# Two banks of one double PSUM tile are read once both are written, and the gate rows and residual pieces are loaded earlier, in the feed-forward block of a two-layer diffusion trunk

## The chip, the cores and the metric

The kernel runs on one core of a Trainium2 chip. The metric is the device time of one execution in microseconds (us). The engines are TensorE (PE), VectorE (DVE), ScalarE (ACT) and GpSimd (POOL); SyncE (SP) issues most of the DMA loads, and ACT's queue issues some.

## The reference

A trunk of two layers works on 512 latent rows and 256 context rows of width 1024. Each layer has mixers, an output projection and a layer norm, and then the block that this change is about:

```python
f = channel_mlp(modulate(x, m[3], m[4]), w_ff1[l], w_ff2[l])     # square(relu(h @ w1)) @ w2, 1024 -> 4096 -> 1024
x = layer_norm_affine(DN_ALPHA * x + m[5] * f, ln2_g[l], ln2_b[l])
```

Here `m[5]` is a gate vector, one value for each of the 1024 columns. Layer 0 does the same for the context rows with a gate of their own; in layer 1 the context rows need no feed-forward block. All of it is float32.

## The kernel before, in words

A float32 matmul is done as three matmuls of rounded halves (`mm3`, line 133: hi·hi, lo·hi, hi·lo), so every operand is split in two: ACT copies the high half, DVE subtracts to get the low half. The names are `hiw`/`low` for weights, `fop` for the halves of an operand of the second matmul, `hh`/`hl` for the normalised input.

**The chunks.** The 4096 hidden columns go in eight chunks of 512. In layer 0 the rows are 768 (latent and context), in layer 1 they are 512. In chunks 0 to 6 the product with `w_ff2` is done by a scheme with seven half-sized products in place of eight: `operands` makes the seven left sides (POOL sums, then `fop` halves by ACT line 1269 and DVE line 1270), `weights` the seven right sides (POOL differences line 1295, halves by ACT line 1290 and DVE line 1291), and `product(i, ...)` multiplies. A product fills HT banks of PSUM, 128x512 each (HT is 3 in layer 0, 2 in layer 1), with six matmuls a bank. Each bank is then added into one or more quadrants of the result, `acc` or `base`, by DVE (line 1340); the first time a quadrant is touched, ACT copies it (line 1343).

**The banks.** Products 0, 2, 4 and 6 use single-bank tiles (`PA`, three buffers). Products 1, 3 and 5 use a double tile `P2` of two banks (two buffers, shared with the `ff1` tiles), and in layer 0 one bank `PF` besides. The framework tracks who reads and writes a tile as a whole: in a double tile, the first matmul into the second bank stands behind the reads of the first.

**The order of the work.** TensorE's order is written by hand. Each letter f is one `ff1` tile of the next chunk (24 matmuls of 512 columns, in layer 0 another 24 of 256 columns), each digit one product:

```python
order = "f01f23f45f6" if c < NCH - 2 else "01f23f456ff"
```

The other engines and the DMA queues run in the order that the framework's scheduler gave them. Each works strictly through its own list: what stands behind a waiting instruction waits too.

**The end of a layer's block (the tail).** After chunk 6 the gate rows are loaded (`rows2(0)`, on ACT's DMA queue, one row spread over 128 partitions) into pool G (four buffers). Then, for each of the six (four) 128x1024 tiles of `acc`: POOL multiplies by the gate (line 1422), DVE adds the residual rows `rawx` (line 1423), loaded from the DRAM copy `xr` into the raw pool (four buffers of 512 KB, which the weights use too). Then chunk 7 is done the plain way: `square` makes `fh`, `fl` from the hidden rows, `ff2_w` loads and splits the last weights of `w_ff2` (lines 163, 166), `ff2_tile` multiplies, DVE takes the bank times the gate (`fft`, line 1366), POOL adds it to `acc` (line 1367), and `done` does the layer norm (lines 181, 343, 345) and, in layer 0, makes the input halves `hh`, `hl` of the next layer, whose first products are `wb`.

Of the kernel before, what the change touches and what calls it, by code (L numbers as in the profile page):

```python
# [9 lines left out]
F32 = mybir.dt.float32  # L10
F32R = mybir.dt.float32r
AF = mybir.ActivationFunctionType
ALU = mybir.AluOpType
# [7 lines left out]
LT = NL // 128  # L21
# [26 lines left out]
class Trunk:  # L48
# [1133 lines left out]
    def ffn(self, l, hL, hC, x, xc, rows2, mod2, done):  # L1182
        nc, A = self.nc, self.A
        w1 = A["w_ff1"][l].rearrange("(k p) n -> p k n", p=128)
        w2 = A["w_ff2"][l].rearrange("(f p) n -> p f n", p=128)
        NCH = DFF // 512
# [7 lines left out]
        def ff1_mm(o, h, t0, W):  # L1194
            t1 = t0 + o.shape[-1]
            for k in range(KT):
                self.mm3(o, W[k], [t[:, t0:t1] for t in h[k]], k == 0, k == KT - 1)
# [4 lines left out]
        def square(r, n):  # L1202
            hi, lo = self.Z("fh"), self.Z("fl")
            nc.scalar.activation(out=hi[:, :n], in_=r[:, :n], func=AF.Square)
            nc.vector.tensor_tensor(out=r[:, :n], in0=r[:, :n], in1=r[:, :n], op=ALU.mult)
            nc.vector.tensor_tensor(out=lo[:, :n], in0=r[:, :n], in1=hi[:, :n].bitcast(F32), op=ALU.subtract)
            return hi, lo

        N = NL + NC if full else NL
        half = N // 2  # L1210
        HT = half // 128

        def ff1_tile(f, spare):

            W = ff1_w(f, spare)
            ps = self.P2("ff1")
            ff1_mm(ps[:, :NL], hL, 0, W)
            if full:
                ff1_mm(ps[:, NL:NL + NC], hC, 0, W)
            r = self.T("relu", 768)  # L1220
            relu(r, 0, ps[:, :N])
            return r
# [57 lines left out]
        def weights(c):  # L1280
# [28 lines left out]
        TO = (("11", "B"), ("12",), ("11",), ("12", "22"), ("B",), ("21", "22"), ("21",)) if full else (  # L1309
            ("11",), ("12",), ("2",), ("22",), ("6",), ("7",), ("21",))  # L1310

        def place(acc, base, q, t):
            if len(q) == 1:
                return base[q][t]
            n = int(q[1]) - 1
            return acc[HT * (int(q[0]) - 1) + t][:, 512 * n:512 * n + 512]

        def product(i, B, left, acc, base, seen):

            if i in (0, 2, 4, 6):
                banks = [self.PA("ff2") for _ in range(HT)]
            else:
                big = self.P2("ff2")
                banks = [big[:, 0:512], big[:, 512:1024]]
                if HT > 2:
                    banks.append(self.PF("ff2"))
            W = next(B)
            for t in range(HT):  # L1330
                ps = banks[t]
                for p in range(2):
                    self.mm3(
                        ps, [h[:, 128 * t:128 * t + 128] for h in left[p][i]],
                        [h[:, p, :] for h in W], p == 0, p == 1,
                    )
                for q in TO[i]:
                    sl = place(acc, base, q, t)
                    if (q, t) in seen:
                        nc.vector.tensor_tensor(out=sl, in0=ps, in1=sl, op=ALU.add)  # L1340
                    else:
                        seen.add((q, t))
                        nc.scalar.activation(out=sl, in_=ps, func=AF.Copy)

        def ff2_w(c, n):
            return [
# [22 lines left out]
        rs = ff1_first()  # L1369

        xr = self.pd.tile([N, D], F32, name=self.nm("xr"), tag=self.nm("xr"))
        for j, t in enumerate(x + (xc or [])):
            nc.sync.dma_start(out=xr[128 * j:128 * j + 128, :], in_=t)
        acc = [self.X([128, 1024], "acc") for _ in range(N // 128)]
        base = {}
# [8 lines left out]
        seen = set()  # L1384
        self.pin = True
        for c in range(NCH - 1):
            B = weights(c)
            rs, nxt = [], []
            order = "f01f23f45f6" if c < NCH - 2 else "01f23f456ff"
            for o in order:  # L1390
                if o != "f":
                    product(int(o), B, left, acc, base, seen)
                    continue
                rs.append(ff1_tile(4 * c + 4 + len(rs), True))
                if c < NCH - 2 and len(rs) % 2 == 0:
                    nxt.append(operands(*rs[-2:]))
            left = nxt
        self.pin = None

        gl, gc = rows2(0)  # L1400

        def plus(o, a):
            nc.vector.tensor_tensor(out=o, in0=o, in1=a, op=ALU.add)
# [9 lines left out]
            plus(c21, p7)  # L1413
            plus(c22, p7)
        for j, t in enumerate(acc):
            raw = self.pr.tile([128, 1024], F32, name=self.nm("rawx"), tag="raw")
            self.load(out=raw, in_=xr[128 * j:128 * j + 128, :])
            for n in range(2):
                if full and (j >= HT or n):
                    sl = t[:, 512 * n:512 * n + 512]  # L1420
                    nc.vector.tensor_tensor(out=sl, in0=sl, in1=base["B"][j % HT], op=ALU.add)
            nc.gpsimd.tensor_tensor(out=t, in0=t, in1=gl if j < LT else gc, op=ALU.mult)
            nc.vector.tensor_tensor(out=t, in0=t, in1=raw, op=ALU.add)
        rows2(1)
        fs = [square(r, N) for r in rs]
        tiles = [(128 * j, t, gl if j < LT else gc) for j, t in enumerate(acc)]
        Ws = [ff2_w(NCH - 1, n) for n in range(2)]
        self.ends = []
# [239 lines left out]
```

## Time and profile before

| what | value |
|---|---|
| median of the 2 runs shown | 1746.6 us (1743.52 to 1749.68) |
| the profiled execution | 1759.88 us, span 1758.0 us |
| busy over the span | PE 86%, DVE 60%, ACT 40%, POOL 29% |
| mean granted TensorE clock | 0.936 of full speed |
| chunks 0 to 6, layer 0 | 450 to 966.6 us |
| tail, layer 0 | 966.6 to 1034.5 us |
| chunks 0 to 6, layer 1 | 1350 to 1699.5 us |
| tail, layer 1 | 1699.5 to 1758 us |

The profiled execution is 13.3 us longer than the median of the runs. TensorE is the busiest engine, so the time goes where its idle time is, and where its clock is below full speed (the two levels are 2.4 and 1.2 GHz; a value between 0.5 and 1 is a mix over the stretch).

### The profile page before, as it was taken

The numbers are of one execution on the slowest core, as the hardware profiler recorded it, in microseconds if no ns is written. First come the engines' busy times: TensorE is split into PE (matmuls) and PEld (weight loads), VectorE is DVE, ScalarE is ACT, GpSimd is POOL, SyncE is SP. The second block draws the span as 40 slices with busy tenths as digits, with TensorE's granted clock in tenths as the row PEclk, the third lists the DMA queues.
The fourth block names the chain that finished last, engine by engine and source line by source line (L and its number), as shares of the span: only waits on it lengthen the run. The fifth ranks groups of instructions, "written<-read, shape, count | busy, mean of one in ns | idle before, by whom it ended". The sixth has DMA issues, their size and how long they took to land.

```text
span 1758.0 us, 23844 instructions
## 1 busy us (share of the span) xinstructions
PE 1511.0 (86%) x9228; PEld 1245.6 (71%) x9228; DVE 1046.3 (60%) x1773; ACT 697.8 (40%) x1267; POOL 507.9 (29%) x422
## 2 busy tenths in 40 slices
PE   5899898999888988988889499988989898888865
PEld 4788777878777777877767377877767676666644
DVE  3394556475545455465554788576565556666567
ACT  4444455335532233233221165355445543343312
POOL 1011442232231213213220631153233432334323
PEclk9999999999998999999989699999989999999987
DMA  8432564542112121121110523245460332322122
GB/s 294 127 111 76 164 199 150 200 155 72 62 46 84 37 60 61 48 60 48 61 60 12 191 97 85 85 157 168 156 210 13 108 95 84 96 74 83 60 72 83
DMA packets 150952, 180.42 MB, mean 103 GB/s; under 512 B 9096, under 2 KB 96568, under 8 KB 150840
## 3 DMA queue, kind: packets, MB, share of 16 engines
q1 hardware_dynamic: 140792, 160.42, 29.0%
q10 hardware_dynamic: 10048, 18.49, 3.1%
q8 instruction: 72, 1.18, 0.3%
q14 instruction: 40, 0.33, 0.1%
HBM read 169.43 MB, written 9.46 MB: 102 GB/s over the span
## 4 chain that ended last, share of the span: by engine, by line
PE 57%; DVE 18%; issue 8%; POOL 7%; ACT 5%; DMA 4%; SPq 0%; POOLq 0%; DVEq 0%; ACTq 0%
PE ff L133 29%; PE wo L133 6%; PE wb L133 3%; DVE acc L1340 3%; POOL raww L1295 3%; DVE fop L1270 2%; DVE low L1291 2%; PE o L133 2%; PE ada L133 2%; PE wa L133 2%; PE pT L189 2%; PE wp L133 2%; DMA wada<-in_w_ada 2%; PE wu L133 2%; ACT hiw L1290 2%
## 5 line engine op out<-in xcount | busy, mean ns | idle before, releaser
L133 PE MATMUL ff<-hiw,fop 128*128 128x512 f32 x980 | 356.4, 430 | 109.5 <-DVE acc L1340 84.0
L133 PEld LDWEIGHTS ff<-hiw,fop 128*128 128x128 f32 x980 | 203.4, 208 | 177.1 <-DVE acc L1340 99.3
L1291 DVE TENSOR_TENSOR low<-raww,hiw 128x1024 fp32r<-128x1024 f32 x98 | 137.4, 1404 | 217.6 <-ACT hiw L1290 217.6
L1295 POOL TENSOR_TENSOR raww<-raww,raww 128x1024 f32<-128x1024 f32 x56 | 142.3, 2542 | 349.9 <-DMA raww<-in_w_ff 117.8
L133 PE MATMUL ff<-hh,hiw 128*128 128x512 f32 (+1 forms) x672 | 239.2, 356 | 0.0
L133 PE MATMUL ff<-hl,hiw 128*128 128x512 f32 (+1 forms) x672 | 238.1, 354 | 0.0
L133 PE MATMUL ff<-hh,low 128*128 128x512 f32 (+1 forms) x672 | 238.0, 354 | 0.0
L1290 ACT ACTIVATE hiw<-raww 128x1024 fp32r<-128x1024 f32 x98 | 103.6, 1059 | 306.5 <-PE ff L133 306.4
L133 PE MATMUL ff<-low,fop 128*128 128x512 f32 x490 | 207.7, 424 | 0.0
L1340 DVE TENSOR_TENSOR acc<-ff,acc 128x512 f32<-128x512 f32 x228 | 152.3, 685 | 67.8 <-PE ff L133 65.0
L133 PEld LDWEIGHTS ff<-hh,hiw 128*128 128x128 f32 x672 | 128.3, 191 | 19.4
L133 PEld LDWEIGHTS ff<-hl,hiw 128*128 128x128 f32 x672 | 128.0, 190 | 19.2
L133 PEld LDWEIGHTS ff<-hh,low 128*128 128x128 f32 x672 | 127.2, 189 | 18.1
L163 ACT ACTIVATE hiw<-raww 128x1024 fp32r<-128x1024 f32 x64 | 67.9, 1061 | 163.7 <-PE ff L133 122.1
L1270 DVE TENSOR_TENSOR fop<-relu,fop 128x384 fp32r<-128x384 f32 (+1 forms) x140 | 80.9, 605 | 65.3 <-ACT fop L1269 65.3
L133 PEld LDWEIGHTS ff<-low,fop 128*128 128x128 f32 x490 | 102.1, 208 | 19.5
L166 DVE TENSOR_TENSOR low<-raww,hiw 128x1024 fp32r<-128x1024 f32 x64 | 87.6, 1369 | 35.1 <-ACT hiw L163 35.1
L548 POOL TENSOR_SCALAR p<-p,rec 128x768 f32<-128x768 f32 (+3 forms) x80 | 63.4, 796 | 140.6 <-DVE rec L547 131.3
L1269 ACT ACTIVATE fop<-relu 128x384 fp32r<-128x384 f32 (+1 forms) x140 | 58.3, 460 | 82.5 <-POOL relu L1277 82.1
L1274 POOL TENSOR_TENSOR fsum<-relu,relu 128x384 f32<-128x384 f32 (+1 forms) x28 | 25.4, 907 | 208.6 <-ACT relu L1261 208.6
L133 PE MATMUL ada<-wada,sc 128*32 128x128 f32 x1536 | 62.8, 302 | 21.0 <-DMA wada<-in_w_ada 21.0
L1200 ACT ACTIVATE relu<-ff 128x768 f32<-128x768 f32 (+2 forms) x76 | 45.4, 606 | 73.9 <-PE ff L133 73.8
(365 smaller groups left out, 3219.9 us busy)
## 6 DMA issues: line engine op xcount, KB each, us to landing
raww<-in_w_ff SPq DMA_DIRECT2D x120, 512.0 KB, 4.1
wada<-in_w_ada SPq DMA_DIRECT2D x96, 512.0 KB, 4.4
rawwo<-in_w_out SPq DMA_DIRECT2D x16, 512.0 KB, 6.4
rawx<-xr SPq DMA_DIRECT2D x10, 512.0 KB, 3.3
rawz<-in_w_ff SPq DMA_DIRECT2D x8, 512.0 KB, 4.8
xr<-x SPq DMA_DIRECT2D x8, 512.0 KB, 7.2
rawwb<-in_w_in SPq DMA_DIRECT2D x12, 256.0 KB, 3.8
gate<-grow ACTq DMA_DIRECT2D x6, 512.0 KB, 7.6
```

Of the source, the lines that this page charges most:

```text
L133: return self.pinned(self.nc.tensor.matmul(out, lhsT, rhs, start=start, stop=stop))
L163: i = nc.scalar.activation(out=hi, in_=raw, func=AF.Copy)
L166: nc.vector.tensor_tensor(out=lo, in0=raw, in1=hi.bitcast(F32), op=ALU.subtract)
L189: return self.pinned(self.nc.tensor.transpose(out, in_, self.ident if ident is None else ident))
L548: nc.gpsimd.tensor_scalar(out=p[:, :keep], in0=p[:, :keep], scalar1=rec, scalar2=1.0, op0=ALU.mult, op1=ALU.mult)
L1200: nc.scalar.activation(out=r[:, a:a + ps.shape[-1]], in_=ps, func=AF.Relu)
L1269: nc.scalar.activation(out=hi, in_=v, func=AF.Copy)
L1270: nc.vector.tensor_tensor(out=lo, in0=v, in1=hi.bitcast(F32), op=ALU.subtract)
L1290: nc.scalar.activation(out=hi, in_=t, func=AF.Copy)
L1291: nc.vector.tensor_tensor(out=lo, in0=t, in1=hi.bitcast(F32), op=ALU.subtract)
L1295: nc.gpsimd.tensor_tensor(out=o, in0=a, in1=b, op=ALU.subtract)
L1340: nc.vector.tensor_tensor(out=sl, in0=ps, in1=sl, op=ALU.add)
```

## The change

First, in products 1, 3 and 5 the first bank is no longer read when it is written: nothing is read after bank 0, and after bank 1 both banks are read, first 0, then 1. The third bank in layer 0 is read as before, and so are the single-bank tiles. Second, the two last `ff1` tiles of chunk 6 load their weights into the raw pool instead of pool G, and the gate rows are loaded right behind the second f of that chunk, with the products 4, 5 and 6 and two f still to come. Third, `square` stands ahead of the gate and residual step; the residual rows come in halves of 128x512 (12 in layer 0, 8 in layer 1; 256 KB each) into pool Z (18 buffers) instead of whole rows into the raw pool; and gate and residual are done half by half.

```diff
-                for q in TO[i]:
-                    sl = place(acc, base, q, t)
-                    if (q, t) in seen:
-                        nc.vector.tensor_tensor(out=sl, in0=ps, in1=sl, op=ALU.add)
...
+                for t2 in (t,) if i % 2 == 0 or t > 1 else ((), (0, 1))[t]:
+                    for q in TO[i]:
+                        sl = place(acc, base, q, t2)
+                        if (q, t2) in seen:
+                            nc.vector.tensor_tensor(out=sl, in0=banks[t2], in1=sl, op=ALU.add)
...
-                rs.append(ff1_tile(4 * c + 4 + len(rs), True))
+                rs.append(ff1_tile(4 * c + 4 + len(rs), c < NCH - 2 or len(rs) < 2))
+                if c == NCH - 2 and len(rs) == 2:
+                    gl, gc = rows2(0)
...
-        gl, gc = rows2(0)
+        fs = [square(r, N) for r in rs]
...
-            raw = self.pr.tile([128, 1024], F32, name=self.nm("rawx"), tag="raw")
-            self.load(out=raw, in_=xr[128 * j:128 * j + 128, :])
             for n in range(2):
+                sl = slice(512 * n, 512 * n + 512)
+                back = self.Z("xr", F32)[:, 0:512]
+                self.load(out=back, in_=xr[128 * j:128 * j + 128, sl])
                 if full and (j >= HT or n):
-                    sl = t[:, 512 * n:512 * n + 512]
-                    nc.vector.tensor_tensor(out=sl, in0=sl, in1=base["B"][j % HT], op=ALU.add)
-            nc.gpsimd.tensor_tensor(out=t, in0=t, in1=gl if j < LT else gc, op=ALU.mult)
-            nc.vector.tensor_tensor(out=t, in0=t, in1=raw, op=ALU.add)
+                    plus(t[:, sl], base["B"][j % HT])
+                nc.gpsimd.tensor_tensor(out=t[:, sl], in0=t[:, sl], in1=(gl if j < LT else gc)[:, sl], op=ALU.mult)
+                plus(t[:, sl], back)
         rows2(1)
-        fs = [square(r, N) for r in rs]
```

TensorE, product 3 of a chunk in layer 0, where its second bank begins (`ff_1364` is the double tile; a minus is before, a plus is the change):

```order
 L133 MATMUL ff_1364_6723<-low_1367_6727,fop_6444 128x512
 L133 MATMUL ff_1364_6723<-hiw_1366_6726,fop_6444 128x512
-L133 MATMUL ff_1364_6723<-hiw_1366_6726,fop_6183 128x512 [waits DVE_49]
+L133 MATMUL ff_1364_6723<-hiw_1366_6726,fop_6183 128x512
 L133 MATMUL ff_1364_6723<-low_1367_6727,fop_6183 128x512
 L133 MATMUL ff_1364_6723<-hiw_1366_6726,fop_6183 128x512
```

The second bank began behind a wait for DVE, and now begins with none; the same holds at all 42 such places (three products, seven chunks, two layers). TensorE's order itself is the same.

DVE at the same product, before (`acc` and the number behind it are quadrants of the result, `ff_1365` is the third bank, `fop` are operands of the next chunk):

```order
L1340 TENSOR_TENSOR acc_4926<-ff_1364_6723,acc_4926 128x512 [waits DVE_49,PE_49]
L1340 TENSOR_TENSOR acc_4929<-ff_1364_6723,acc_4929 128x512
L1270 TENSOR_TENSOR fop_6675<-relu_6539,fop_6675 128x384 [waits Activation_49]
L1270 TENSOR_TENSOR fop_6678<-relu_6663,fop_6678 128x384 [waits Activation_49]
L1270 TENSOR_TENSOR fop_6681<-fsum_6667,fop_6681 128x384 [waits Activation_49]
L1270 TENSOR_TENSOR fop_6684<-fsum_6667,fop_6684 128x384 [waits Activation_49]
L1340 TENSOR_TENSOR acc_4927<-ff_1364_6723,acc_4927 128x512 [waits DVE_49,PE_49]
L1340 TENSOR_TENSOR acc_4930<-ff_1364_6723,acc_4930 128x512
L1270 TENSOR_TENSOR fop_6687<-relu_6539,fop_6687 128x384 [waits Activation_49]
L1270 TENSOR_TENSOR fop_6690<-relu_6663,fop_6690 128x384 [waits Activation_49]
L1340 TENSOR_TENSOR acc_4928<-ff_1365_6724,acc_4928 128x512 [waits DVE_49,PE_49]
L1340 TENSOR_TENSOR acc_4931<-ff_1365_6724,acc_4931 128x512
```

And the same rows of the change:

```order
L1342 TENSOR_TENSOR acc_4926<-ff_1364_6723,acc_4926 128x512 [waits DVE_49,PE_49]
L1342 TENSOR_TENSOR acc_4929<-ff_1364_6723,acc_4929 128x512
L1342 TENSOR_TENSOR acc_4927<-ff_1364_6723,acc_4927 128x512 [waits DVE_49]
L1342 TENSOR_TENSOR acc_4930<-ff_1364_6723,acc_4930 128x512
L1270 TENSOR_TENSOR fop_6675<-relu_6539,fop_6675 128x384 [waits Activation_49]
L1270 TENSOR_TENSOR fop_6678<-relu_6663,fop_6678 128x384 [waits Activation_49]
L1342 TENSOR_TENSOR acc_4928<-ff_1365_6724,acc_4928 128x512 [waits DVE_49,PE_49]
L1342 TENSOR_TENSOR acc_4931<-ff_1365_6724,acc_4931 128x512
L1270 TENSOR_TENSOR fop_6681<-fsum_6667,fop_6681 128x384 [waits Activation_49]
L1270 TENSOR_TENSOR fop_6684<-fsum_6667,fop_6684 128x384 [waits Activation_49]
L1270 TENSOR_TENSOR fop_6687<-relu_6539,fop_6687 128x384 [waits Activation_49]
L1270 TENSOR_TENSOR fop_6690<-relu_6663,fop_6690 128x384 [waits Activation_49]
```

The four adds of the double tile stand together, and four operand halves have moved behind the adds of the third bank.

SP's queue at the end of layer 0's chunks, before (`raww` of 128x8x128 are the last `ff1` weights, of 128x2x512 the `w_ff2` weights of chunk 7):

```order
L116 DMA raww_1590_8306<-in_w_ff 128x8x128 [waits DMAHW1_49,DVE_49]
L116 DMA rawx_8424<-xr_4919 128x1024 [waits DVE_49,Pool_49]
L116 DMA raww_1595_8363<-in_w_ff 128x8x128 [waits DMAHW4_49,DMAHW0_49,DVE_49]
L116 DMA rawx_8429<-xr_4919 128x1024 [waits DVE_49,Pool_49]
L116 DMA rawx_8434<-xr_4919 128x1024 [waits DMAHW2_49,DVE_49]
L116 DMA rawx_8439<-xr_4919 128x1024 [waits DMAHW3_49,DVE_49]
L116 DMA rawx_8445<-xr_4919 128x1024 [waits DMAHW7_49,DMAHW0_49,DVE_49]
L116 DMA rawx_8451<-xr_4919 128x1024 [waits DMAHW1_49,DVE_49]
L116 DMA raww_1618_8481<-in_w_ff 128x2x512 [waits DMAHW2_49,DVE_49]
L116 DMA raww_1621_8487<-in_w_ff 128x2x512 [waits DMAHW3_49,DVE_49]
```

And of the change, from the third of the four `w_ff2` tiles on (`rawwbz` and `rawwb` are input weights of the next layer, `xr` on the left a residual half):

```order
L116 DMA raww_1630_8517<-in_w_ff 128x2x512 [waits DMAHW6_49,DMAHW4_49,DVE_49]
L116 DMA raww_1633_8523<-in_w_ff 128x2x512 [waits DMAHW7_49,DMAHW5_49,DVE_49]
L116 DMA rawwbz_8529<-in_w_in 128x2x256 [waits DMAHW0_49,DVE_49]
L116 DMA rawwbz_8529<-in_w_in 128x2x256
L116 DMA rawwbz_8540<-in_w_in 128x256 [waits DMAHW1_49,DVE_49]
L116 DMA rawwbz_8540<-in_w_in 128x256
L116 DMA rawwb_8926<-in_w_in 128x2x256 [waits DMAHW4_49,DMAHW2_49,DVE_49]
L116 DMA rawwb_8926<-in_w_in 128x2x256 [waits DMAHW3_49]
L116 DMA rawwb_8933<-in_w_in 128x2x256 [waits DMAHW6_49,DMAHW5_49,DVE_49]
L116 DMA rawwb_8933<-in_w_in 128x2x256 [waits DMAHW7_49]
L116 DMA xr_8444<-xr_4919 128x512 [waits DMAHW0_49,PE_49]
L116 DMA xr_8448<-xr_4919 128x512 [waits DMAHW1_49,PE_49]
```

The residual loads stood ahead of the four `w_ff2` tiles; now they stand behind them and behind eight loads of the next layer's weights. In layer 1 nothing of a next layer stands between.

## Rows read from the trace of the kernel before

**Rows 1.** Waits by engine and line, whole span: total us, times, longest.
```profile
POOL acc L1422 <- DMA gate<-grow: 130.4, 2, 78.8
```
**Rows 2.** Tile `ff` (the PSUM banks): who waited for it, us and times.
```profile
  PE ff L133: 91.5, 42
```
**Rows 3.** TensorE's waits, 450 to 966.6 us (layer 0, chunks 0 to 6).
```profile
PE ff L133 <- DVE acc L1340: 50.4, 19, 3.9
PE ff L133 <- ACT acc L1343: 5.0, 2, 2.6
```
**Rows 4.** TensorE's waits, 1350 to 1699.5 us (layer 1, chunks 0 to 6).
```profile
PE ff L133 <- DVE acc L1340: 33.6, 18, 2.8
PE ff L133 <- DVE fop L1270: 9.5, 6, 2.4
PE ff L133 <- ACT fop L1269: 5.8, 6, 2.5
PE ff L133 <- ACT acc L1343: 2.5, 3, 1.1
```
**Rows 5.** TensorE's timeline, layer 0: start, length, instruction [idle before it <- releaser].
```profile
573.67 0.39 PE L133 MATMUL ff<-hh,hiw 128*128 128x512 f32 x1
...
582.03 0.40 PE L133 MATMUL ff<-hiw,fop 128*128 128x512 f32 x1
...
586.13 0.39 PE L133 MATMUL ff<-hh,hiw 128*128 128x512 f32 x1
...
603.19 0.50 PE L133 MATMUL ff<-hiw,fop 128*128 128x512 f32 x1 [3.11 <-DVE acc L1340]
```
**Rows 6.** DVE's timeline just ahead of 603.19 us.
```profile
600.12 1.22 DVE L1291 TENSOR_TENSOR low<-raww,hiw 128x1024 fp32r<-128x1024 f32 x1
...
602.45 0.68 DVE L1340 TENSOR_TENSOR acc<-ff,acc 128x512 f32<-128x512 f32 x1
```
**Rows 7.** Windows: stretch, us, busy PE, PEld, DVE, ACT, POOL (instructions), clock, DMA share, GB/s.
```profile
603.20:678.60 75.40, 67.66 (x319) 56.40 (x319) 40.44 (x56) 23.75 (x33) 19.42 (x13) 0.93 0.19 57
603.20:607.60 4.40, 4.40 (x12) 3.52 (x13) 2.81 (x3) 0.10 (x1) 0.57 (x1) 0.61 0.37 117
607.60:620.10 12.50, 12.50 (x68) 10.77 (x67) 4.38 (x5) 3.60 (x5) 1.24 (x2) 1.00 0.20 53
1454.40:1505.60 51.20, 43.76 (x181) 34.58 (x181) 31.34 (x40) 20.56 (x33) 17.98 (x12) 0.97 0.27 82
```
**Rows 8.** TensorE's timeline in layer 0's tail: first `w_ff2` matmul, first use of `hl`.
```profile
988.18 0.80 PE L133 MATMUL ff<-hiw,fh 128*128 128x512 f32 x1 [21.62 <-ACT hiw L163]
...
1034.53 0.79 PE L133 MATMUL wb<-wbz,hl 128*128 128x512 f32 x1 [0.96 <-DVE hl L389]
```
**Rows 9.** Windows of the two tails, columns as in Rows 7.
```profile
966.60:1034.50 67.90, 39.15 (x154) 30.52 (x154) 57.54 (x71) 19.40 (x32) 39.47 (x23) 0.77 0.46 152
1699.50:1758.00 58.50, 24.61 (x96) 18.91 (x96) 41.37 (x53) 11.54 (x14) 26.58 (x17) 0.74 0.29 99
```
**Rows 10.** DVE's groups, 966.6 to 1034.5 us: busy us, mean ns.
```profile
L1423 DVE TENSOR_TENSOR acc<-acc,rawx 128x1024 f32<-128x1024 f32 x6 | 17.7, 2998 | 2.2 <-POOL acc L1422 2.2
```
**Rows 11.** Lines 1423, 1422 and 1340, whole span: ns min/median/max.
```profile
L1423 DVE TENSOR_TENSOR acc<-acc,rawx x10: 1212/3354/3372, 973.5 to 1717.2; 128x1024 f32<-128x1024 f32 x10
L1422 POOL TENSOR_TENSOR acc<-acc,gate x10: 2336/3317/3328, 970.7 to 1711.8; 128x1024 f32<-128x1024 f32 x10
...
L1340 DVE TENSOR_TENSOR acc<-ff,acc x228: 675/684/693, 468.8 to 1689.5; 128x512 f32<-128x512 f32 x114
```
**Rows 12.** SP's queue in layer 0's tail: start, us until the last of the group is issued.
```profile
983.42 8.07 SPq L116 DMA_DIRECT2D raww<-in_w_ff  x4
...
996.10 3.68 SPq L116 DMA_DIRECT2D rawwb<-in_w_in  x4
```
**Rows 13.** TensorE's timeline in layer 1's tail, first and last matmul.
```profile
1714.40 0.80 PE L133 MATMUL ff<-hiw,fh 128*128 128x512 f32 x1 [14.91 <-ACT hiw L163]
...
1741.60 0.39 PE L133 MATMUL ff<-hiw,fl 128*128 128x512 f32 x1
```

More of the change, by code (lines that the diff above doesn't have):

```diff
@@ L1336, in product @@
                     )
-                for q in TO[i]:
-                    sl = place(acc, base, q, t)
-                    if (q, t) in seen:
-                        nc.vector.tensor_tensor(out=sl, in0=ps, in1=sl, op=ALU.add)
-                    else:
-                        seen.add((q, t))
-                        nc.scalar.activation(out=sl, in_=ps, func=AF.Copy)
+                for t2 in (t,) if i % 2 == 0 or t > 1 else ((), (0, 1))[t]:
[3 more added lines that the diff above has]
+                            nc.vector.tensor_tensor(out=sl, in0=banks[t2], in1=sl, op=ALU.add)
+                        else:
+                            seen.add((q, t2))
+                            nc.scalar.activation(out=sl, in_=banks[t2], func=AF.Copy)
         def ff2_w(c, n):
```

## The prediction

> **What bounds the kernel now.** I read the table of waits first, then what waited for the banks, TensorE's waits stretch by stretch, its timeline in one chunk, and the windows of chunks and tails. TensorE is busy 86% of the span, so the question is where the rest goes.
>
> In the chunks, TensorE stood idle 42 times, 91.5 us in all, at a bank that had still to be read [rows 2]. 42 is three double-tile products in seven chunks in two layers: each such product pays once, at its second bank. In layer 0 these are 50.4 + 5.0 = 55.4 us in 21 waits [rows 3], in layer 1 33.6 + 2.5 = 36.1 us in 21 [rows 4]. The wait is longer than the read of one bank, because DVE is in a backlog: ahead of the matmul at 603.19, which had waited 3.11 us [rows 5], DVE did a weight half of 1.22 us and other adds before the awaited read of 0.68 us at 602.45 [rows 6].
>
> The waits cost a second time, by the clock. Behind the wait at 603.19 the granted clock was 0.61 for 4.4 us, a mix of the two levels, and then 1.00 [rows 7].
>
> In the tails TensorE stands still longest in one place: 21.62 us in layer 0 [rows 8] and 14.91 us in layer 1 [rows 13], both ended by a weight half `hiw` whose load was late. Its cause is further back: POOL waited 78.8 us (and in both layers together 130.4) for the gate rows [rows 1], which were asked for only when all chunks were over; the residual adds waited for POOL, and the four raw buffers that these held stood ahead of the `w_ff2` loads, the first of them issued at 983.42 [rows 12].
>
> **The sum, part by part.** It is made against the profiled 1759.88 us, which is 13.3 us above the median of the runs.
>
> *Chunks of layer 0.* None of the 42 second banks waits any more. What a chunk costs without stalls comes from the timeline: an f takes 582.03 − 573.67 = 8.36 us, a product 586.13 − 582.03 = 4.10 us [rows 5], so four f and seven products take 62.1 us. The chunk from 603.2 took 75.40 us [rows 7]: 13.3 us more, of which 55.4 / 7 = 7.9 us are waits and some 5.4 us the clock. Seven chunks: 55.4 us of waits and 7 × 5.4 = 37.8 us of clock, −93 us. What must hide the moved reads: DVE's 40.4 us of work per chunk [rows 7] now has to fit into 62 us in place of 75, a load of 65%. Four adds of a double tile stand together and push `fop` halves back by up to four adds, 2.7 us; behind products 1, 3 and 5 comes an f of 8.36 us that needs none of them. I take the full gain; if that cover fails, half of it is gone, 46 us, and a small stall that stays could keep the clock loss of 37.8 us.
>
> *Chunks of layer 1.* A product has 12 matmuls and an f 24 of the same 0.228 us (4.10 us for 18), so 2.73 and 5.46 us, and a chunk 41.0 us, against 51.2 [rows 7]. Of the 10.2 us between, the bank waits are 36.1 / 7 = 5.2, the operand waits on `fop` (9.5 + 5.8) / 7 = 2.2 [rows 4], and the rest, 2.8 us, the clock (0.97 in the mean). The operand waits stay: no double-tile product lies between the last f of a chunk and the operands that the next one's first product waits for. Whether the clock still falls behind them alone, the trace does not show, because both stand in the same windows; so the clock gives back between 0 and 2.8 us per chunk, and I take the half. −36.1 − 7 × 1.4 = −46 us, between −36 and −56.
>
> *Tail of layer 0.* From the end of the last f (966.6) to the first use of the next layer's `hl` (1034.5) it takes 67.9 us, and DVE is busy for 57.5 of them [rows 9]; TensorE is busy 39. Gate rows now land during the last products, and POOL's six multiplies, 2.34 us each when undisturbed [rows 11], fit into the 16.7 us of the last two f. The first three `w_ff2` tiles are loaded and split before the last f ends, and TensorE can begin some 2 us after it. Then DVE sets the end: it loses three weight halves (3 × 1.22 = 3.7 us [rows 6]), and its residual adds fall from 17.7 us [rows 10] to 12 × 0.61 = 7.3 us if POOL is done, half of the 1.21 us that an undisturbed add of twice the size took [rows 11]. That leaves 57.5 − 3.7 − 10.4 = 43.4 us, from about 2.5 us behind the last f on (relu and square on ACT), so not before 46.
>
> What speaks against it is SP's queue. The residual halves stand behind all `w_ff2` tiles and eight loads of the next layer; the last `w_ff2` load needs the last raw buffer, some 2 us after the last f. At 0.9 us for an issue (3.68 us for four [rows 12]) twenty more take 18 us, and the last half lands about 22 us after the last f; DVE then still has some 28 us to do (some 16 of its 43 lie ahead of the last half), so 50. Between 46 and 62 I take 51, the nearest to the load's bound: −17 us. If the halves also come late one by one and DVE waits for each of them while the `fft` reads stand behind, half of that 22 us comes on top, −6; with no lateness it is −22. Nothing of the edit lets this tail end later than before except a stall of DVE by over 17 us.
>
> *Tail of layer 1.* No next layer's loads stand in the way. TensorE begins some 2 us after the last f in place of 14.9, its eight banks take 12 × 0.228 × 8 = 21.9 us, and from its last matmul to the end of the span it is 1758.0 − 1741.6 = 16.4 us [rows 13]. That gives 40.5 in place of 58.5 us [rows 9]; DVE's work, 41.4 us before, falls by 3.7 and by some 6 to 32, and does not bind. −18 by this; −17 with a little for late halves; bounds −11 and −21.
>
> *What costs nothing.* The two last `ff1` weights go through the raw pool as all others did before; these loads run ahead of their use. The eight more residual loads lie on a queue that is otherwise waiting. The last `fh` and the last `hiw` on ACT now stand ahead of the layer norm rows, which are wanted only after the first `acc` tile is complete.
>
> Sum: −93 − 46 − 17 − 17 = −173 us, so 1587 us for an execution like the profiled one, and 1746.6 × (1587 / 1759.9) = **1575 us** for the median.
>
> **Two rules set against the trace.** DVE's residual add took 1.21 us once and 3.35 us in the median, with POOL's multiply at 3.32 us beside it, against 2.34 at the least [rows 11]: the two slowed each other. The Trainium skill, SBUF — State Buffer, section "SBUF: two separate sides", says that VectorE and GpSimd share a port pair as an exclusive lock, held for a whole instruction, when a VectorE operation has two SBUF inputs and GpSimd reads SBUF too. By that rule the gain on DVE hangs on POOL being idle, and every residual add that meets POOL's additions costs its full wait; at 1.68 us for each of the 12 halves, half of 3.35, the layer 0 tail would gain 4 us in place of 17. The trace agrees in kind, and the bank reads, which have one PSUM input, show no such slowing: 228 of them took between 675 and 693 ns [rows 11].
>
> DVE starts a late read only when what stands ahead in its list is done [rows 6]. The Trainium skill, TensorE: Matmul & The Clock Gate, section "Architectural detail: the array is 16× 32×32, not 1× 128×128", says the same as a rule: ScalarE and VectorE are strict first-in first-out. By it, an add that now waits for the second bank holds up every weight half behind it, which is the first rival below.
>
> **The rivals.**
>
> *DVE's backlog comes back as late operands.* The bunched adds wait for the second bank, one bank's 1.37 us later than before, and the `low` halves and `fop` stand behind them. If TensorE reaches these before DVE, half of the gain in the chunks goes, −47 − 23 − 34 = −104: 1656 us, or 1643 for the median. For it: DVE's backlog ahead of 603.19, and the operand waits of layer 1 [rows 4]. Against it: 65% load in layer 0; but in layer 1 31.3 us in 43 to 45 are 70% [rows 7].
>
> *The change does not do what it says in the chunks.* The waits move to the next read of a bank, and only the tails gain: −34, 1726 us, or 1713 for the median. Against it: the program has no wait at these 42 places any more.
>
> *Slower: the wait moves to the next user of a double tile.* The tile is let go only when four adds have run behind the second bank, and there are two such tiles for products and `ff1` tiles together. If each of the 42 successors waited as long as the longest wait of before, 3.9 us [rows 3], that would be 164 us in place of 91.5, with the clock as before: +72 − 34 = +38, 1798 us, or 1784 for the median. Against it: the f between two such products uses the other tile for 8.36 us (layer 1: 5.46), and four adds take 2.7. It decides from a DVE backlog of some 6 us in layer 0, 3 in layer 1, and reaches no change where the new waits and the tails cancel, at 3 us a place.
>
> **How the numbers follow.** The forecast, with its own range of 1550 to 1620 (at the low end −93 − 56 − 22 − 21 = −192 us, 1556 for the median, and a little below; at the high end both tails and layer 1 at their small ends and half of layer 0's clock loss kept, −74 − 36 − 6 − 11 = −127, 1620): 0.70. Late operands, 1620 to 1670: 0.23. Only the tails: 0.04. Slower: 0.03. The range leaves out at most 2 in 10, so it goes from **1550** to **1640**, near the middle of the first rival's band. Faster by over 2% (35 us, about what a measurement of this kernel tells from no change) holds the forecast, the first rival and a part of the second: 0.95; within 2% 0.03; slower by over 2% 0.02.
>
> **What would show it.** Right: the waits of TensorE for `acc` reads are gone or a few us; a middle chunk of layer 0 takes 62 to 64 us with a clock near 1.00, one of layer 1 43 to 45; the first `w_ff2` matmul begins within 4 us of the last f; POOL's wait for the gate rows ends before the last f does. Wrong: new rows in which TensorE waits for `low`, `fop` or a double tile in the chunks; residual adds of DVE that wait for their load by over 10 us; a first use of `hl` more than 60 us after the last f.

## The result, and the profile after

The changed kernel took 1598.95 us in the median of its two runs, against 1746.6 us: ratio 0.9155, 95% interval 0.9051 to 0.9258. In four later runs, beside seven of the kernel before (median 1757.4 us), it took 1601.6 us in the median, ratio 0.911, interval 0.9084 to 0.9136. The forecast was 1575 us, a ratio of 0.902, with a range up to 1640.

The profiled execution of the changed kernel took 1595.83 us, span 1594.0, that is 164 us less than the profiled one before. The waits of TensorE come first, from the table of waits (engine, line, what it waited for: total us, times, longest):

```profile
PE ada L133 <- DMA wada<-in_w_ada: 21.6, 11, 11.3
PE hT L189 <- ACT xn L357: 15.6, 2, 13.5
PE ff L133 <- DVE fl L1206: 11.9, 4, 4.4
PE ff L133 <- DVE fop L1270: 11.4, 9, 1.4
PE ff L133 <- ACT fop L1269: 9.6, 7, 3.7
...
PE ff L133 <- ACT hiw L163: 1.1, 1, 1.1
```

No row says any more that TensorE waited for an `acc` read; before, these were the 91.5 us of [rows 2]. The 36.5 us in which TensorE had waited for `hiw` at the tails' beginnings [rows 8, 13] are down to 1.1. New is `fl`, the low half of the last hidden rows, with 11.9 us, and at the end of layer 0's tail TensorE now stands still for 13.5 us for `xn`, the normalised rows of the next layer.

Windows of the changed kernel (stretch, us, busy PE, PEld, DVE, ACT, POOL, clock, DMA share, GB/s): a middle chunk of layer 0, two of layer 1, the whole chunk stages, the two tails, and the stretch from the end of the first tail's window to the last `wq` matmul of layer 1.

```profile
515.00:577.10 62.10, 62.10 (x320) 53.33 (x319) 40.79 (x56) 23.66 (x33) 19.69 (x13) 1.00 0.23 68
1330.30:1375.20 44.90, 42.93 (x181) 34.77 (x181) 32.65 (x40) 20.61 (x34) 18.00 (x12) 0.96 0.32 94
1375.20:1418.50 43.30, 41.34 (x181) 33.60 (x181) 32.41 (x40) 20.52 (x34) 18.01 (x12) 1.00 0.32 98
441.30:872.00 430.70, 427.87 (x2181) 365.73 (x2180) 288.12 (x378) 168.07 (x236) 138.94 (x85) 1.00 0.23 70
1234.30:1545.60 311.30, 292.54 (x1234) 236.73 (x1235) 221.06 (x270) 145.93 (x235) 120.97 (x79) 0.97 0.32 97
872.00:932.40 60.40, 39.74 (x157) 30.90 (x155) 52.87 (x84) 16.38 (x30) 30.12 (x21) 0.79 0.47 152
1545.60:1594.00 48.40, 24.48 (x96) 18.92 (x94) 39.87 (x59) 8.25 (x11) 23.73 (x17) 0.78 0.21 76
932.40:989.70 57.30, 57.25 (x279) 47.18 (x278) 50.38 (x119) 40.01 (x82) 10.64 (x14) 0.98 0.33 96
```

The same chunk stages, and the same stretch behind the first tail, in the kernel before:

```profile
445.50:966.60 521.10, 464.49 (x2180) 386.50 (x2178) 277.99 (x377) 165.97 (x234) 119.98 (x74) 0.93 0.18 54
1346.50:1699.50 353.00, 301.02 (x1233) 237.06 (x1233) 213.07 (x271) 142.72 (x231) 112.65 (x74) 0.96 0.27 79
1034.50:1099.50 65.00, 60.97 (x278) 50.10 (x278) 54.52 (x126) 40.37 (x83) 11.09 (x16) 0.92 0.32 95
```

In the middle chunk of layer 0 TensorE is busy for all of its 62.1 us at full clock, where it took 75.4 [rows 7]. In layer 1 a chunk still has some 2 us of idle time, and in one of the two shown the clock is 0.96. In the tails the clock is below 0.8 and DVE is busy most of the time.

Stage by stage, from the first product of a layer to its last f, and so on (before; after; difference):

| stage | before | after | difference | forecast |
|---|---|---|---|---|
| up to the first product of layer 0 | 445.5 | 441.3 | −4.2 | 0 |
| chunks of layer 0 | 521.1 | 430.7 | −90.4 | −93 |
| last f to the last `wq` matmul of layer 1 | 132.9 | 117.7 | −15.2 | −17 (tail) |
| from there to layer 1's first product | 247.0 | 244.6 | −2.4 | 0 |
| chunks of layer 1 | 353.0 | 311.3 | −41.7 | −46 |
| tail of layer 1 | 58.5 | 48.4 | −10.1 | −17 |

The mark at layer 1's first product is that product's fourth matmul, behind a wait of 1.0 us for `fop`. The mark behind the third stage is the last of the next layer's `wq` matmuls, at 1099.5 us before and at 989.7 after. At the first use of `hl`, the mark of the prediction, only 7.5 us are won (67.9 to 60.4), and the rest by `wq`. By the first use of `hl` DVE had begun the first step of the layer norm (line 343) for five of six tiles before and for all six after, the last one (line 345) for three before and for four after. From there to the last `wq` TensorE was idle for 4.0 us before and for none after, and its busy time fell by another 3.7 us with the clock (0.92 before, 0.98 after).

TensorE's timeline of the changed kernel, layer 0's tail and then layer 1's (start, length, instruction [idle before it <- releaser]):

```profile
871.96 0.40 PE L133 MATMUL ff<-hiw,fh 128*128 128x512 f32 x1
...
877.00 0.80 PE L133 MATMUL ff<-hiw,fl 128*128 128x512 f32 x1 [3.04 <-DVE fl L1206]
...
881.08 0.79 PE L133 MATMUL ff<-hiw,fl 128*128 128x512 f32 x1 [2.43 <-DVE fl L1206]
...
928.32 1.54 PE L189 MATMUL hT<-ident,xn 128*128 128x128 f32 x6 [13.46 <-ACT xn L357]
...
1545.62 0.39 PE L133 MATMUL ff<-low,fh 128*128 128x512 f32 x1
...
1551.81 0.67 PE L133 MATMUL ff<-hiw,fl 128*128 128x512 f32 x1 [4.44 <-DVE fl L1206]
...
1555.35 0.80 PE L133 MATMUL ff<-hiw,fl 128*128 128x512 f32 x1 [2.01 <-DVE fl L1206]
```

The `w_ff2` matmuls now follow the last f without a gap, where they had come 21.62 and 14.91 us later [rows 8, 13]. Then they stop twice in each layer for `fl`. DVE's timeline shows what stood ahead of it in layer 0:

```profile
871.70 2.32 DVE L166 TENSOR_TENSOR low<-raww,hiw 128x1024 fp32r<-128x1024 f32 x1
873.94 2.02 DVE L1205 TENSOR_TENSOR relu<-relu 128x768 f32<-128x768 f32 x1
875.99 0.96 DVE L1206 TENSOR_TENSOR fl<-relu,fh 128x768 fp32r<-128x768 f32 x1
...
884.08 0.69 DVE L1407 TENSOR_TENSOR acc<-acc,xr 128x512 f32<-128x512 f32 x1 [1.48 <-DMA xr<-xr]
```

A weight half and the square, which take 1.2 and 0.95 us when POOL is idle, took 2.32 and 2.02, and POOL's timeline has three gate multiplies there:

```profile
869.55 5.59 POOL L1426 TENSOR_TENSOR acc<-acc,gate 128x512 f32<-128x512 f32 x3 [0.63 <-DVE acc L1407]
```

Each of these instructions of DVE reads two SBUF operands, like the residual adds that took longer beside POOL before [rows 11]. The forecast had POOL done at this place; it was not, because the later multiplies waited for adds of DVE (line 1407). DVE's groups from 872 to 932.4 us:

```profile
L1407 DVE TENSOR_TENSOR acc<-acc,xr 128x512 f32<-128x512 f32 x12 | 9.5, 820 | 1.5 <-DMA xr<-xr 1.5
L166 DVE TENSOR_TENSOR low<-raww,hiw 128x1024 fp32r<-128x1024 f32 x2 | 3.5, 1768 | 0.0
```

The residual halves, which the prediction took for the danger, held DVE up for 1.48 us in all, and their adds took 0.82 us each, between the 0.61 of the sum and the 1.68 that the prediction named for adds that all meet POOL.

### The profile page after: what moved, and what is told of

The parts are those of the page before. It is cut to its first block, busy times and chain, and to the rows that moved or that the text cites. A ratio compares the mean times of both kernels' runs of the same rounds, so it can differ in the third digit from the quotient of the medians.

```text
span 1594.0 us, 23889 instructions
## 1 busy us (share of the span) xinstructions
PE 1457.4 (91%) x9228; PEld 1217.4 (76%) x9228; DVE 1051.5 (66%) x1783; ACT 696.4 (44%) x1267; POOL 521.8 (33%) x432
## 4 chain that ended last, share of the span: by engine, by line
PE 72%; DVE 13%; POOL 5%; ACT 4%; issue 3%; DMA 3%; SPq 0%; POOLq 0%; DVEq 0%; ACTq 0%
PE ff L133 41%; PE wo L133 6%; PE wb L133 3%; PE o L133 2%; PE ada L133 2%; PE wa L133 2%; PE pT L189 2%; DMA wada<-in_w_ada 2%; DVE acc L1407 2%; PE wu L133 2%; PE wp L133 2%; PE wq L133 2%; PE sm L133 2%; POOL raww L1295 2%; DVE fop L1270 1%
## 5 line engine op out<-in xcount | busy, mean ns | idle before, releaser
L133 PE MATMUL ff<-hiw,fop 128*128 128x512 f32 x980 | 318.8, 397 | 20.9 <-DVE fop L1270 11.4
L1291 DVE TENSOR_TENSOR low<-raww,hiw 128x1024 fp32r<-128x1024 f32 x98 | 147.5, 1507 | 142.5 <-ACT hiw L1290 142.5
L133 PEld LDWEIGHTS ff<-hiw,fop 128*128 128x128 f32 x980 | 186.0, 191 | 66.1 <-DVE fop L1270 15.8
L133 PE MATMUL ff<-low,fop 128*128 128x512 f32 x490 | 193.6, 395 | 0.0
L1342 DVE TENSOR_TENSOR acc<-ff,acc 128x512 f32<-128x512 f32 x228 | 148.0, 684 | 18.7 <-PE ff L133 16.6
L166 DVE TENSOR_TENSOR low<-raww,hiw 128x1024 fp32r<-128x1024 f32 x64 | 92.7, 1448 | 25.5 <-ACT hiw L163 25.5
L133 PEld LDWEIGHTS ff<-low,fop 128*128 128x128 f32 x490 | 93.4, 191 | 18.3
L133 PEld LDWEIGHTS ada<-wada,sc 128*32 128x32 f32 x1536 | 42.3, 117 | 35.5 <-DMA wada<-in_w_ada 14.3
```

The source lines that it names most:

```text
L133: return self.pinned(self.nc.tensor.matmul(out, lhsT, rhs, start=start, stop=stop))
L166: nc.vector.tensor_tensor(out=lo, in0=raw, in1=hi.bitcast(F32), op=ALU.subtract)
L1291: nc.vector.tensor_tensor(out=lo, in0=t, in1=hi.bitcast(F32), op=ALU.subtract)
L1342: nc.vector.tensor_tensor(out=sl, in0=banks[t2], in1=sl, op=ALU.add)
```

## The experiments

**The bank reads alone (e1).** The kernel before with only the reading order of the change.

```diff
+                for t2 in (t,) if i % 2 == 0 or t > 1 else ((), (0, 1))[t]:
+                    for q in TO[i]:
...
+                            nc.vector.tensor_tensor(out=sl, in0=banks[t2], in1=sl, op=ALU.add)
```

> Only the reading order of products 1, 3 and 5 is changed; gate rows, residual rows and square stay as before. Theory A (the 42 waits come from the double tile being tracked as one, and the two parts of the change are independent): layer 0's chunks fall to about 431 us and layer 1's to about 311 us as in the changed kernel, both tails stay at 68 and 58 us, so the time is that of the changed kernel plus what its tails gained (15 + 10 us): about 1624 us, ratio to before 0.93. Rival B (part of the chunk gain came from the earlier gate rows and the raw buffers): 1640 us or more, with waits left in chunk 6.

Measured: 1622.9 us beside 1758.2, ratio 0.9233 (0.9186 to 0.9280). TensorE has no wait for `acc`. The tail of layer 0 is as before, as its timeline shows:

```profile
872.77 0.28 PE L133 MATMUL ff<-hh,low 128*128 128x256 f32 x1
...
894.68 0.80 PE L133 MATMUL ff<-hiw,fh 128*128 128x512 f32 x1 [21.63 <-ACT hiw L163]
```

The last `wq` matmul comes at 1005.4, 132.4 us after the last f, as before (132.9). No bank wait is left in chunk 6 either, so rival B is out, and theory A holds, to 1 us of the forecast time.

**The tails alone (e2).** The changed kernel with the reading order of before.

```diff
-                for t2 in (t,) if i % 2 == 0 or t > 1 else ((), (0, 1))[t]:
...
+                for q in TO[i]:
+                    sl = place(acc, base, q, t)
```

> Only gate rows, residual pieces and square are changed; the banks are read as before. Theory A: all 42 bank waits (about 91 us) and the clock losses behind them stay, the tails fall by 15 and 10 us: about 1722 us, ratio 0.986. Rival B (parts interact): if the tails gain only when the chunks run without backlog, under 10 us, 1737 us or more; if the tail part also helps the chunks, under 1710 us.

Measured: 1731.2 us beside 1758.2, ratio 0.9831 (0.9773 to 0.9889). The bank waits are all there, as the table of waits shows:

```profile
PE ff L133 <- DVE acc L1341: 86.6, 37, 6.6
...
PE ff L133 <- ACT acc L1344: 7.5, 5, 2.6
```

The forecast ratio, 0.986, lies in the interval, which leaves a gain of 1.1 to 2.3%, and the two parts add up: −7.7% and −1.7% against −8.9% for both, within the intervals. So theory A stands, though a small interaction is not ruled out, and one shows in the trace: the tails are 18.3 and 13.3 us shorter than before, but layer 0's chunks 4.2 us longer, and the longest bank wait has grown from 3.9 us [rows 3] to 6.6, in chunk 6, where DVE's adds now run while POOL does gate multiplies (from 936.08 on).

```profile
943.75 0.79 PE L133 MATMUL ff<-hiw,fop 128*128 128x512 f32 x1 [6.56 <-DVE acc L1341]
```

**Two tiles in place of one, layer 1 (e3).** The kernel before; the reads stay where they were.

```diff
-                banks = [big[:, 0:512], big[:, 512:1024]]
+                banks = [big[:, 0:512], big[:, 512:1024] if HT > 2 else self.PF("ff2")]
```

> The kernel before, with one edit: in layer 1 the second bank of products 1, 3 and 5 is a single-bank tile of its own, so that the reads stay where they were (each bank right after it is written) and no tile holds two banks. Theory A (the wait is a matter of tracking the two banks as one tile, not of reading early or late): the 21 waits of layer 1 vanish, its chunk stage falls from 353 to about 311 us, about 1705 us, ratio 0.976. Rival (what helps is that the reads are bunched and later, so DVE works in another order): the waits stay or turn into waits at the next bank, 1735 us or more.

Measured: 1714.0 us beside 1758.2, ratio 0.9740 (0.9698 to 0.9783), 44.2 us less in the medians and 46.3 between the profiled executions. The table of waits holds layer 0's bank waits alone, and layer 1's chunks take as long as in the changed kernel to 0.3 us from the same mark (the window shown begins 1.0 us ahead of it):

```profile
PE ff L133 <- DVE acc L1340: 50.4, 19, 3.9
```

```profile
1341.56:1654.10 312.54, 293.17 (x1234) 236.70 (x1233) 219.73 (x273) 143.84 (x235) 114.33 (x75) 0.96 0.29 90
```

So the waits of layer 1 came from holding two banks in one tracked tile, not from the reads being early: with two tiles the old reading order does as well as the new one. Layer 0 was not tried this way.

**One product of the three as before (e8).** The changed kernel, with product 1 reading each bank when it is written.

```diff
-                for t2 in (t,) if i % 2 == 0 or t > 1 else ((), (0, 1))[t]:
+                for t2 in (t,) if i % 2 == 0 or i == 1 or t > 1 else ((), (0, 1))[t]:
```

> The changed kernel, with product 1 reading its banks as before (14 of the 42 waits come back: the first of each chunk, 2.4 to 3.6 us in layer 0, 1.1 to 2 us in layer 1). Theory A (each wait costs itself and some 1.8 us of clock behind it in layer 0, and in layer 1 the clock that the fop waits already cost): 7 x 4.9 + 7 x 2 = 48 us more. Rival B (the clock falls only where several waits come close together): the waits alone, some 34 us more, chunk clock 1.00 in layer 0. Rival C (the wait is short when DVE has less backlog, because the other two products no longer bunch up): under 25 us.

Measured: 1654.5 us beside 1757.4, ratio 0.9414 (0.9387 to 0.9442), 52.8 us above the changed kernel run beside it. TensorE's timeline, its table of waits and the windows of the chunk behind one such wait:

```profile
517.55 0.50 PE L133 MATMUL ff<-hiw,fop 128*128 128x512 f32 x1 [3.11 <-DVE acc L1342]
```

```profile
PE ff L133 <- DVE acc L1342: 30.5, 12, 3.6
...
PE ff L133 <- ACT acc L1345: 3.5, 2, 2.4
```

```profile
517.50:584.50 67.00, 63.85 (x319) 54.28 (x319) 40.17 (x56) 23.65 (x33) 19.53 (x13) 0.97 0.21 63
517.50:522.00 4.50, 4.45 (x13) 3.57 (x14) 2.88 (x4) 0.53 (x1) 0.63 (x1) 0.67 0.33 110
522.00:584.50 62.50, 59.40 (x307) 50.71 (x305) 37.29 (x53) 23.12 (x33) 18.90 (x12) 0.99 0.20 60
```

The wait of 3.11 us is back to the hundredth. The chunk takes 67.0 us, 4.9 more than 62.1: the wait and 1.8 us for the clock, which was 0.67 in the 4.5 us behind it. Of the 52.8 us, 34.0 are the 14 waits, and the rest is near 14 times 1.3. Theory A holds, 5 us above its 48: in this run the clock added 55% to the waits, though only one of them falls in each chunk, which rules out rival B. Less backlog on DVE (rival C) does not shorten the wait.

**The order of layer 1 (e5).** The changed kernel, one f earlier in chunks 0 to 5 of layer 1.

```diff
-            order = "f01f23f45f6" if c < NCH - 2 else "01f23f456ff"
+            order = ("f01f23f45f6" if full else "f01f23f4f56") if c < NCH - 2 else "01f23f456ff"
```

> The changed kernel with product 5 and the last f exchanged in chunks 0 to 5 of layer 1 (f01f23f4f56 in place of f01f23f45f6), so that 10.9 us in place of 8.2 lie between the last f and the next chunk's product 0. Theory A (what stays of layer 1's excess, 44.9 and 43.3 us a chunk against 41.0, are the waits for fop behind the last f, 2 us a chunk, and the clock that falls after them): these waits vanish in five chunks, a chunk takes 41 to 42 us with clock 1.00, 10 to 18 us less in all. Rival (the two f so close make a wait of their own, for the double tile or for weights): no gain, or up to 10 us more.

Measured: 1583.4 us, ratio 0.9001 (0.8978 to 0.9023), 18.2 us below the changed kernel beside it, which is the next run. A chunk of layer 1 (window):

```profile
1330.00:1371.00 41.00, 41.00 (x183) 33.95 (x182) 32.45 (x41) 20.93 (x34) 18.18 (x12) 1.00 0.34 104
```

TensorE is busy throughout at full clock, with DVE at 79%: 41.0 us is the prediction's chunk without stalls. So what the change left in such a chunk was the lateness of `fop` behind the last f, and the clock after it. The gain lies at the upper end of theory A's 10 to 18 us. The rival's wait for weights shows once, in the first chunk, where the two f now stand closer:

```profile
1268.69 0.50 PE L133 MATMUL ff<-hh,hiw 128*128 128x512 f32 x1 [1.63 <-ACT hiw L163]
```

**The changed kernel again (e6)**, as the level for these runs.

> The changed kernel itself, beside the other three on the same chip: 1594 to 1602 us as first measured where the kernel before takes 1747 to 1758; ratio 0.905 to 0.92. It is the level that the other three are compared with.

Measured: 1601.6 us beside 1757.4, ratio 0.911 (0.9084 to 0.9136).

**The square on ACT (e4).** The changed kernel; DVE makes only the low half of the last hidden rows.

```diff
-            nc.scalar.activation(out=hi[:, :n], in_=r[:, :n], func=AF.Square)
-            nc.vector.tensor_tensor(out=r[:, :n], in0=r[:, :n], in1=r[:, :n], op=ALU.mult)
+            nc.scalar.activation(out=r[:, :n], in_=r[:, :n], func=AF.Square)
+            nc.scalar.activation(out=hi[:, :n], in_=r[:, :n], func=AF.Copy)
```

> The changed kernel; of the last chunk's hidden rows ACT makes the square and its copy, and DVE only the low half (one DVE instruction less for each of the four tiles, one ACT instruction more). Theory A (TensorE's 11.9 us of waits for fl in the tails are DVE's in-order queue): these waits fall to 4 to 8 us, the time by 4 to 8 us, about 1593 us. Rival (ACT sets it: the relu and the square of the last f come late in any case): fl waits unchanged or longer, 1599 us or up to 1605.

Measured: 1595.5 us beside 1758.2, ratio 0.9079 (0.9039 to 0.9120). By itself that is not told apart from the changed kernel's 0.911, so the time decides nothing here. In the trace layer 1's tail (window) took 43.3 us in place of 48.4, and its waits for `fl` and `fh` together 2.2 us in place of 6.5:

```profile
1556.70:1600.00 43.30, 22.57 (x97) 17.69 (x96) 34.30 (x53) 8.88 (x12) 24.38 (x19) 0.82 0.24 85
```

Layer 0's tail, up to the last `wq`, took 114.9 us in place of 117.7; its waits for `fl` and `fh` fell from 5.5 to 2.2, and 2.9 us of waits for `fft` are new. Theory A holds for the waits, whose sum fell from 11.9 us to 4.4 with `fh` counted in.

**Both edits (e7, and e11 as its repeat)**, square and order.

> Both edits: the square on ACT for the last chunk, and the exchanged order in layer 1. If they are independent, the sum of both: e4's tail of layer 1 (43 us in place of 48) and 10 to 18 us in layer 1's chunks, 13 to 23 us below the changed kernel run beside it.

> The kernel of e7 again as the level for the other two: ratio to before 0.895 to 0.900.

Measured: 1579.8 us beside 1757.4, ratio 0.8981 (0.8964 to 0.8998), 21.8 us below the changed kernel; on another chip 1582.8 beside 1754.5, ratio 0.9007 (0.8970 to 0.9044). Both gains together lie within the 13 to 23 us of the sum. Over the exchanged order alone the square is worth 3.7 us in the medians, within the noise (0.9001 and 0.8981, with intervals that overlap).

**The start of chunk 6, from two sides (e9, then e10).** Both build on the kernel of e7.

```diff
+            if c == NCH - 3:
+                order = "f01f23ff456"
```

> The kernel of e7, with the last two f of chunk 5 ahead of the products 4, 5 and 6 in both layers (f01f23ff456), so that chunk 6, which begins with product 0, finds its operands: TensorE's waits for fop there were 3.8 + 1.4 us in layer 1 and 1.2 in layer 0. Theory A (they are lateness behind the last f alone): 3 to 7 us less than e7, ratio to before 0.894 to 0.897. Rival (two f in a row stand still for the double tile of product 3 or for weights): no gain or up to 5 us more.

Measured: 1577.9 us, ratio 0.8999 (0.8956 to 0.9041); not told apart from e7's 0.9007. The waits for `fop` are gone from chunk 6, but two others are there, for reads of a bank. The longer one, with DVE's timeline ahead of it:

```profile
815.45 0.76 PE L133 MATMUL ff<-hiw,fop 128*128 128x512 f32 x1 [4.23 <-DVE acc L1342]
```

```profile
805.82 2.48 DVE L1342 TENSOR_TENSOR acc<-ff,acc 128x512 f32<-128x512 f32 x4
808.22 3.88 DVE L1270 TENSOR_TENSOR fop<-relu,fop 128x384 fp32r<-128x384 f32 x2
...
814.62 0.68 DVE L1342 TENSOR_TENSOR acc<-ff,acc 128x512 f32<-128x512 f32 x1
```

Products 4, 5, 6 and 0 stand in a row with no f between. Product 0 needs the bank that product 6 filled first, and the read of that bank, at 814.62, stands in DVE's list behind operand halves. Neither theory had this: it is DVE's backlog, which the prediction's first rival is built on, but it shows as a late read of a single-bank tile and not as a late operand. Against the repeat of e7 layer 1's chunks became 5.2 us shorter in the traces and layer 0's 6.9 us longer, so what the covered `fop` waits gave was taken back.

```diff
+                "01f23f456ff" if full else "f01f23f456f")
```

> The kernel of e7, with chunk 6 of layer 1 beginning with an f (f01f23f456f): the same waits are covered from the other side, but only one f instead of two stands between the last product and the end. Theory A: the fop waits vanish, 4 to 6 us less, given back in part because the last bank reads, gates and residual halves now fall into the tail: within 3 us of e7. Rival (the tail is not bound by them): 4 to 6 us less than e7.

Measured: 1575.2 us, ratio 0.8969 (0.8932 to 0.9007), not told apart from e7 either. The waits for `fop` are gone from layer 1's chunk 6, and layer 1's tail has a longer wait for `fl`:

```profile
1539.59 0.80 PE L133 MATMUL ff<-hiw,fl 128*128 128x512 f32 x1 [7.18 <-DVE fl L1206]
```

Against the repeat of e7 layer 1's chunks are 7.7 us shorter in the traces and its tail 4.3 us longer, so a part is given back, as theory A had it. The medians lie 7.5 us apart, within the noise, and don't decide between theory A and its rival.

## Why the prediction was right

*The signs.* All four signs of being right came: no wait for `acc`, chunks of 62.1 and of 44.9 and 43.3 us, `w_ff2` matmuls right behind the last f, and gate rows that landed ahead of it (POOL's multiplies began at 847.4 in layer 0). Of the signs of being wrong, two came in a weak form: the chunks have new waits of TensorE (1.3 us for `fop` in layer 1's first chunk, 1.6 us for weight halves in layer 0's), and the first use of `hl` came 60.4 us after the last f, just over the 60 that the prediction had named.

*The waits.* All 42 are gone, as the sum had it. That they hang on the tile, and not on when the reads happen, is shown for layer 1 by the two tiles, which remove 21 of them with the reads unmoved.

*The clock.* The second charge for each wait, 5.4 us a chunk in layer 0, came back in full: the middle chunk is 62.1 us at clock 1.00. Over the seven chunks TensorE's busy time fell by 36.6 us, where 37.8 was forecast. Restoring one wait in three brings back 1.8 us a chunk, a third.

*The cover for the moved reads.* DVE at 66% of the chunk (40.8 of 62.1) kept up. The prediction's reason was the f behind products 1, 3 and 5. Behind product 5 it turned out not to be needed: in chunk 6 of the changed kernel, and with e5's order in chunks 0 to 5 of layer 1, product 6 follows product 5 directly, and no wait for a bank appears. One appears in e9, with 4.2 us, where four products stand in a row while DVE has operand halves to make, and it is at a bank whose read the change does not move. So the first rival was wrong for the order as it is, and not because DVE is never late; that an f is what hid the moved reads is argued and not shown.

*Layer 1's chunks* gained 41.7 in place of 46 us. The term that was mis-sized is the operand waits, taken as unchanged. From the mark on they were 15.8 us (the 15.3 of [rows 4] and 0.5 just ahead of that window) and became 18.8, from the table of waits of the changed kernel, 1234.2 to 1545.6 us, less 1.0 that stands ahead of the mark:

```profile
PE ff L133 <- DVE fop L1270: 10.2, 8, 1.4
PE ff L133 <- ACT fop L1269: 9.6, 7, 3.7
```

That is 3.0 us more: one of them, 1.3 us, falls in the first chunk, where the matmuls ahead of it had run at a lower clock before and came no earlier than the operand (that matmul stands 5.6 us behind the mark now and 5.7 before), and the last chunk's are longer by 1.5. The remaining 1.3 us are the clock, of which 8.6 us came back in place of 9.8 (41.7 = 36.1 − 3.0 + 8.6). e5 shows that most of what stayed was the lateness of `fop` and the clock behind it: with these waits gone from five chunk ends the time fell by 18.2 us.

*The tail of layer 0* gained 15.2 in place of 17, and that the two are close is luck. At the prediction's own mark, the first `hl`, it gained 7.5. The term that was mis-sized is DVE's work up to there, 52.9 us and not 43.4: among it, by the lines of the two traces, are about 4.6 us more layer norm than before, 2.9 for a second square and low half that still fell behind the last f, 2.3 for a second weight half and a slower first one, and 2.2 for residual adds of 0.82 us in place of 0.61, while POOL's multiplies ran on to 875. The residual halves themselves came in time. The other 7.7 us were won behind that mark, where the sum had nothing: 4.0 of idle time and 3.7 of clock.

*The tail of layer 1* gained 10.1 in place of 17: the step that failed is "TensorE begins some 2 us after the last f" and then runs through. It began at once, but stood still for 4.44 and 2.01 us for `fl`, in DVE's list behind the adds of the last combination and weight halves, and its clock fell again (0.78 over the tail). The end, from the last matmul on, took 17.9 us in place of 16.4. With the square on ACT the tail took 43.3 us, 15.2 less than before and 1.8 above the forecast 41.5, so these waits are most of what was missing.

*From profile to median.* The sum was −173 against one profiled execution, and −164 were measured between two, of which 6.6 lie in stretches that the change doesn't touch. The ratio to the median of two runs, 1746.6 us, made it 1575; with 21 more runs of the kernel before, the medians were 1758.2, 1757.4 and 1754.5, so the two were low ones, and the profiled 1759.9 is near the usual level. In ratios, 0.902 was forecast and 0.911 measured: 16 us, mostly layer 1's chunks and tail.

## What to carry to other kernels

When TensorE waits at the second bank of a tile for a reader of the first, ask whether the wait is one of data or only of how tiles are tracked; a tile of its own for each bank, or reads behind the last write, remove it. The clock gives something back besides: here TensorE's busy time in the chunks fell by 36.6 us beside 55.4 us of waits in layer 0, and by 8.5 beside 36.1 in layer 1, where other waits stayed. Before moving reads later, look for what stands between them and the next user of their banks: an f of 5 to 8 us stood there in most cases here, and where four products came in a row a wait for DVE appeared, at another bank. And when an early load lets an engine start at once, price the next thing that it needs: here TensorE no longer waited 15 to 22 us for weights, but 5.5 to 6.5 us for a low half in DVE's queue.

## What the runs showed of the hardware that was not expected

DVE instructions took longer beside POOL instructions that have nothing to do with them: in the tail a weight half of 1.22 us took 2.32 and a square of 0.95 took 2.02 beside gate multiplies, and in e9 two operand halves, 0.55 us each when alone, took 3.88 together beside weight differences:

```profile
806.59 5.09 POOL L1295 TENSOR_TENSOR raww<-raww,raww 128x1024 f32<-128x1024 f32 x2
```

It holds over the trace of the changed kernel from 440 us on, counting the rows of a single instruction: 98 low halves of a 128x1024 weight (two SBUF operands) that overlapped no POOL instruction took 1.21 to 1.23 us, and the 57 that did took 1.21 to 3.41, in the median some 1.8. Of the bank adds, which have one PSUM operand, 58 overlapped POOL and took 0.68 to 0.69 us, as they do alone. No run takes POOL's work away, so this is a pattern of the traces and not an experiment.

And a single wait of 3.1 us, once in a chunk that takes 62 us without it, was followed by 4.5 us at a mean granted clock of 0.67.
